# Two network blocks on one core: convolution taps on TensorE column groups, score masks added by VectorE

## The chip, the cores and the metric

The kernel runs on one core of one Trainium2 chip. Its time is device microseconds of one execution; three runs of the kernel before gave 2316.55, 2317.32 and 2319.4 us, and the median, 2317.32 us, is the figure that the change is compared with. Besides the timed runs one execution was profiled, and all durations below come from it.

## The reference, cut to what matters

The program takes 256 tokens of width 1024 through four layers. In the first two, each token mixer is a depthwise convolution of 31 taps over 512 channels beside an attention of 8 heads with a relative bias; a dense feed-forward net and a net of 8 experts follow. The last two layers have a differential attention (a), a sparse attention on the 64 best keys (b), and a compressed, selected and windowed attention (c). What the change touches:

```python
# first block, per layer l
z = a * sigmoid(g)                                     # 256 tokens x 512 channels
z = depthwise_conv(z, conv_w[l], left pad 30) + conv_b[l]   # 31 taps per channel
z = silu(layernorm(z, ln_g, ln_b))
s = einsum(q, k) * 64**-0.5 + rel_bias[clip(key - query)]   # 8 heads, chunks of 64
p = softmax(where(valid, s, -1e30));  o = p @ v

# second block, per layer i
p = softmax(where(mask, q @ k.T, -1e30));  o = p @ v   # mask: causal, or the chosen keys
hid = gelu(einsum("bnlgd,ldf->bngf", blocks, w1))      # compressing net, for keys and for values
kc, vc = hid @ w2
```

## The kernel before, in words

All tensors of one token mixer live on chip; weights stream from HBM once, 1 MB at a time, into four raw tiles, and ScalarE and VectorE split each into two parts (`split`, L176 to L181) so that three products in `mm3` (L183 to L186) give float32 accuracy. SyncE issues all loads in one queue in order; a load waits there until a raw tile is free, and everything behind it waits too. A scheduler fixes the order of the instructions of each engine when the program is built, so an engine stands still when its next instruction is not ready.

`mix1` (from L487) is the token mixer of the first two layers. It projects the gated half (ca, cg), then k, q and v, while in layer 0 the modulation of later parts (`ada` loads, L294, and VectorE's sums, L299) runs between. `gated` writes the convolution's input `zp`, channels on partitions, four tiles of 128 channels. Of the 31 taps of each of the four channel tiles, the table `NPE` gives some to TensorE: 0, 0, 16 and 31 in layer 0, and 0, 0, 0 and 31 in layer 1. A tap on TensorE is a product with a diagonal matrix `dg` that ScalarE makes (L584, L585); a tap on VectorE is one multiply and add over 256 tokens (L569). So 78 taps are products and 170 are VectorE's.

The attention goes through the 8 heads in four pairs. `pair_scores` issues the scores (L611, two heads on the two halves of the rows), adds the bias as a product with a matrix that reverses 128 rows (`flip`, L619), takes the row maximum (L626) and the exponential (L627). The bias tile has one buffer, so the bias of the next pair is loaded (L598) once this pair's has been read; the masked corners are filled by GpSimd (L601, L602). `pair_out` transposes and multiplies with v: the two heads' outputs stand in the two halves of the columns (`po`, L649, L650). `ln` (L689 on) and `wo_unit` finish the mixer.

`block2` (from L1245) is one of the last two layers. `scores` (L1323) makes the scores of two heads and adds the mask as a bf16 product with the identity (L1332 causal, L1334 chosen keys); `softmax_e` (L1313) takes maximum and exponential. The compressing net (L1642) multiplies, for keys and then for values, 16 stationary tiles of 32 columns with `w1`. Pieces of the other matrix products (`fill`) are put between, so TensorE has work while a softmax runs.

The lines of the convolution on TensorE:

```python
A.activation(dg, ident, AF.Copy, scale=cw[:, i, j : j + 1])
T.matmul(st["cps", i][:, :S], dg, zp[:, i, j : j + S], start=(j == 0), stop=(j == npe[i] - 1))
```

Of the kernel before, what the change touches and what calls it, by code (L numbers as in the profile page):

```python
# [24 lines left out]
KT = 8  # L25
# [7 lines left out]
NPE = ((0, 0, 16, 31), (0, 0, 0, 31))  # taps of the convolution on TensorE, by layer and channel tile  # L33
# [3 lines left out]
# columns of the packed per-partition vectors  # L37
# [27 lines left out]
# columns of the second block's w_in  # L65
# [8 lines left out]
def kernel(ctx: ExitStack, tc: tile.TileContext, I: dict, out: bass.AP, dbg=None, upto=99):  # L74
# [3 lines left out]
    # ------------------------------------------------------------- pools  # L78
# [15 lines left out]
    # --------------------------------------------------------- constants  # L94
# [14 lines left out]
    identb = const.tile([P, P], BF16, name="identb")  # L109
    G.tensor_copy(identb, ident)  # L110
    # additive causal mask of a diagonal block: key (free) after query (partition)
# [3 lines left out]
    # the permutation that reverses 128 rows  # L115
    flip = const.tile([P, P], F32, name="flip")
    G.memset(flip, 0.0)
    G.affine_select(flip, flip, pattern=[[1, P]], compare_op=ALU.not_equal, fill=1.0, base=-127, channel_multiplier=1)
    # strictly upper ones: row token before column token
# [22 lines left out]
    ahead = {}  # weights whose loads were started early  # L142
# [47 lines left out]
    def fill(n=1):  # L190
        """Emits the next pieces of matrix products that wait for nothing here."""
# [9 lines left out]
    later = []  # what follows a product, once the next piece's matrix products are out  # L201
# [69 lines left out]
    def transpose4(src, cols):  # L271
        """PSUM [128, 512] with the transposes of src[:, t, cols[i]] at i*256 + t*128."""
# [54 lines left out]
    def mod_parts(l, accp):  # L327
        """Closures of pieces of the six parts of the modulation, by part; each part fills its entry of the dict."""
# [21 lines left out]
    def square(c, ts=(0, 1)):  # L350
        """The sums of squares of one half of x's columns, as soon as that half is done."""
# [8 lines left out]
    def rstd_cols(name, ts=(0, 1)):  # L360
        """1/sqrt(mean(x^2)+eps) of the token tiles ts, each as its own column."""
# [14 lines left out]
    def rsqrt_cols(v, name, ts=(0, 1)):  # L376
        """As rsqrt, of v[:, 0, 0:2], for a short chain: each column by itself with per-partition scalars."""
# [17 lines left out]
    def mod_first(m, accp):  # L395
        """The first norm's shift (on TensorE) and scale (on VectorE) by quarters of the columns, as norm_mod asks for them."""
# [51 lines left out]
    def norm_mod(pool, name, Ac, Bc, before=None):  # L448
        """K-major (x*rstd)*A+B in two parts."""
        rstd, sq = rstd_cols(name)  # L450
        xn = nrm.tile([P, 2, D], F32, tag="xn", name=name + "xn")
# [6 lines left out]
        hT = [pool.tile([P, KT, S], F32R, tag="hT" + "hl"[i], name=name + "hl"[i]) for i in range(2)]  # L458
# [22 lines left out]
    def split_psum(dst, sl, ps):  # L481
        """Both parts of a PSUM result into K-major (or any) tiles dst = [hi, lo]."""
# [3 lines left out]
    def mix1(l, mp, m, fillers, before=None):  # L486
        w_in = I["w_in"][l]  # L487
        npe = NPE[l]
# [10 lines left out]
        # --- gated half for the convolution  # L499
        cv = mp.tile([P, 4, S], F32, tag="cv", name=f"cv{l}")  # L500
        zp = mp.tile([P, 4, S + TAPS - 1], F32, tag="zp", name=f"zp{l}")
        cw = vc(f"cw{l}").rearrange("p (a j) -> p a j", a=4)

        def gated(psg):
# [5 lines left out]
            G.memset(zp[:, :, 0 : TAPS - 1], 0.0)  # L510
            for i in range(0, 4, 2):
                ps = transpose4(z, [i * P, (i + 1) * P])
                A.activation(
                    zp[:, i : i + 2, TAPS - 1 :], ps.rearrange("p (a b) -> p a b", a=2), AF.Identity, scale=0.5
# [3 lines left out]
        grp("cg", 512, gated)  # L518

        # --- queries, keys and values  # L520
# [30 lines left out]
        for i in range(0, 4, 2):  # L551
            ps = transpose4(st["k"], [i * P, (i + 1) * P])
            A.activation(kT[:, i : i + 2, :].rearrange("p a b -> p (a b)"), ps, AF.Identity, scale=vc(f"kg{l}"))
            ps = transpose4(st["q"], [i * P, (i + 1) * P])
            V.tensor_scalar(
                qT[:, i : i + 2, :].rearrange("p a b -> p (a b)"), ps, vc(f"qg{l}"), 0.125, op0=ALU.mult, op1=ALU.mult
            )

        # --- depthwise convolution: some channel tiles on VectorE, the others as diagonal matrices on TensorE
        def conv_v(q):  # L560
            """A third of VectorE's taps, each tap over the channel tiles in turn."""
            todo = [(i, j) for j in range(TAPS) for i in range(4) if j >= npe[i]]
            for i, j in todo[len(todo) * q // 3 : len(todo) * (q + 1) // 3]:
                if j == npe[i]:
                    V.tensor_scalar(
                        cv[:, i, :], zp[:, i, j : j + S], cw[:, i, j : j + 1], vc(f"cb{l}", i, 1), op0=ALU.mult, op1=ALU.add
                    )
                else:
                    V.scalar_tensor_tensor(  # L569
                        cv[:, i, :], zp[:, i, j : j + S], cw[:, i, j : j + 1], cv[:, i, :], op0=ALU.mult, op1=ALU.add  # L570
                    )
            if q == 2:
                for i in range(4):
                    if 0 < npe[i] < TAPS:
                        V.tensor_tensor(cv[:, i, :], cv[:, i, :], st["cps", i][:, :S], op=ALU.add)

        def conv_t(q):
            """A third of TensorE's taps."""
            todo = [(i, j) for i in range(4) for j in range(npe[i])]
            for i, j in todo[len(todo) * q // 3 : len(todo) * (q + 1) // 3]:  # L580
                if j == 0:
                    st["cps", i] = mmps(f"cvp{l}{i}")
                dg = mp.tile([P, P], F32, tag="dg", name=f"dg{l}{i}{j}", bufs=4)
                A.activation(dg, ident, AF.Copy, scale=cw[:, i, j : j + 1])  # L584
# [1370 lines left out]
```

## Time and profile before

| what | value |
|---|---|
| median of three runs | 2317.32 us (2316.55 to 2319.4) |
| span of the profiled execution, first to last instruction | 2314.4 us |
| mean granted TensorE clock | 0.990 |
| TensorE busy, matmul | 2240.5 us, 97% of the span |
| VectorE busy | 1836.1 us, 79% |
| ScalarE busy | 1427.7 us, 62% |
| GpSimd busy | 19.5 us, 1% |
| HBM read | 579.37 MB |

The profiled execution's own time is not listed apart from its span; the span is 2.9 us below the median of the timed runs, which is what lies before the first and after the last instruction together with the difference between executions. Busy time is the time in which an engine worked on something, overlaps counted once. A float32 product shows in the trace as two records on TensorE and two weight loads; a product of one part by one part (`mm3`) and a transpose as one.

### The profile page before, as it was taken

The numbers are of one execution on the slowest core, as the hardware profiler recorded it, in microseconds if no ns is written. First come the engines' busy times: TensorE is split into PE (matmuls) and PEld (weight loads), VectorE is DVE, ScalarE is ACT, GpSimd is POOL, SyncE is SP. The second block draws the span as 40 slices with busy tenths as digits, with TensorE's granted clock in tenths as the row PEclk, the third lists the DMA queues.
The fourth block names the chain that finished last, engine by engine and source line by source line (L and its number), as shares of the span: only waits on it lengthen the run. The fifth ranks groups of instructions, "written<-read, shape, count | busy, mean of one in ns | idle before, by whom it ended". The sixth has DMA issues, their size and how long they took to land. (4 is left out here: it accounts for less than half of the span.)

```text
span 2314.4 us, 28960 instructions
## 1 busy us (share of the span) xinstructions
PE 2240.5 (97%) x10546; PEld 1762.8 (76%) x10546; DVE 1836.1 (79%) x2875; ACT 1427.7 (62%) x2251; POOL 19.5 (1%) x67
## 2 busy tenths in 40 slices
PE   7998998998999999999999999999999999999998
PEld 4776877777877777777778777777777777777776
DVE  7988787887988888888888888986766667766676
ACT  4465344567677767677777767676565546565554
POOL 0000000000000000000000000000000000000000
PEclk9999999999999999999999999999999999999999
DMA  9747886526999999999999999995444346444332
GB/s 337 275 130 280 301 309 225 182 77 218 348 342 337 341 341 360 344 330 343 366 340 348 342 348 357 337 349 199 146 149 147 110 144 186 146 145 140 134 123 91
DMA packets 273452, 582.38 MB, mean 252 GB/s; under 512 B 21644, under 2 KB 41228, under 8 KB 273302
## 3 DMA queue, kind: packets, MB, share of 16 engines
q1 hardware_dynamic: 273302, 580.46, 71.0%
q8 instruction: 85, 1.39, 0.2%
q14 instruction: 65, 0.53, 0.1%
HBM read 579.37 MB, written 1.05 MB: 251 GB/s over the span
## 5 line engine op out<-in xcount | busy, mean ns | idle before, releaser
L299 DVE SCALAR_TENSOR_TENSOR acc<-ada,cact,acc 128x1024 f32<-128x1024 f32 x80 | 102.3, 1280 | 0.9
L483 ACT CAST at<-t 128x512 fp32r<-128x512 f32 x56 | 32.9, 587 | 86.7 <-PE t L1103 86.7
L569 DVE SCALAR_TENSOR_TENSOR cv<-zp,vec,cv 128x256 f32<-128x256 f32 x164 | 70.7, 476 | 0.0
L484 DVE TENSOR_TENSOR at<-t,at 128x512 fp32r<-128x512 f32 x56 | 38.4, 685 | 15.8 <-ACT at L483 15.7
L1320 ACT ACTIVATE ec<-sc,nmc 128x128 f32<-128x128 f32 (+1 forms) x64 | 26.5, 417 | 27.5 <-DVE nmc L1319 25.9
L356 ACT ACTIVATE sqj<-x 128x512 bf16<-128x512 f32 x36 | 22.5, 625 | 29.4 <-DVE x L479 10.6
L585 PE MATMUL cvp<-zp,dg 128*128 128x256 f32 x156 | 39.1, 391 | 0.0
L584 ACT ACTIVATE dg<-ident,vec 128x128 f32<-128x128 f32 x78 | 27.4, 399 | 18.2 <-DVE x L479 14.7
L585 PEld LDWEIGHTS cvp<-zp,dg 128*128 128x128 f32 x156 | 28.9, 193 | 5.4 <-ACT dg L584 0.9
L1063 ACT ACTIVATE gh<-g,mcol,mcol 128x256 f32<-128x256 f32 x32 | 18.2, 570 | 17.9 <-PE g L1053 17.9
L427 PE MATMUL mq<-ada,cact 128*1 128x256 f32 x64 | 17.0, 427 | 9.9 <-DMA ada<-in_w_ada_dram 9.9
L1319 DVE TENSOR_REDUCE nmc<-sc 128x1 f32<-128x128 f32 (+1 forms) x64 | 20.6, 353 | 5.8 <-ACT ec L1320 3.3
L1053 PEld LDWEIGHTS g<-pm,xnt 128*128 128x128 f32 x128 | 20.4, 206 | 4.3 <-issue 2.0
L1053 PE MATMUL g<-pm,xnt 128*128 128x256 f32 x128 | 21.3, 299 | 1.9 <-DVE pm L1045 1.9
L1319 DVE TENSOR_REDUCE nma<-sa 128x1 f32<-128x128 f32 (+1 forms) x32 | 10.4, 351 | 16.0 <-PE sa L1332 13.6
L1127 ACT ACTIVATE yh<-y,ws 128x512 fp32r<-128x512 f32 x14 | 8.9, 685 | 20.9 <-PE y L186 20.9
L427 PEld LDWEIGHTS mq<-ada,cact 128*1 128x1 f32 x64 | 5.6, 91 | 19.9 <-ACT sqj L356 9.3
L619 PE MATMUL s<-bias,flip 128*128 128x128 f32 (+1 forms) x64 | 15.8, 367 | 4.3 <-POOL bias L601 3.7
L627 ACT ACTIVATE sbig<-s,nm 128x128 f32<-128x128 f32 (+1 forms) x32 | 13.2, 415 | 9.6 <-DVE nm L626 9.4
L1147 DVE TENSOR_TENSOR yacc<-yacc,sc 128x512 f32<-128x512 f32 x28 | 19.0, 679 | 0.0
L1320 ACT ACTIVATE eb<-sb,nmb 128x128 f32<-128x128 f32 (+1 forms) x32 | 13.1, 417 | 9.2 <-DVE nmb L1319 8.7
L1347 DVE TENSOR_SCALAR ec<-ec,smc 128x128 f32<-128x128 f32 x64 | 18.1, 313 | 0.8
(4855 smaller groups left out, 8315.6 us busy)
## 6 DMA issues: line engine op xcount, KB each, us to landing
ada<-in_w_ada_dram SPq DMA_DIRECT2D x48, 1024.0 KB, 6.9
bias<-in_rel_bias_dram SPq DMA_DIRECT2D x8, 256.0 KB
x<-in_x_dram SPq DMA_DIRECT2D x1, 1024.0 KB, 4.9
ca0k0r<-in_w_in_dram SPq DMA_DIRECT2D x1, 1024.0 KB
ca0k4r<-in_w_in_dram SPq DMA_DIRECT2D x1, 1024.0 KB
cg0k0r<-in_w_in_dram SPq DMA_DIRECT2D x1, 1024.0 KB
cg0k4r<-in_w_in_dram SPq DMA_DIRECT2D x1, 1024.0 KB, 5.1
k0k0r<-in_w_in_dram SPq DMA_DIRECT2D x1, 1024.0 KB
```

The source lines that it names most:

```text
L299: V.scalar_tensor_tensor(acc, raw[:, k * D : (k + 1) * D], cact[:, k0 + k : k0 + k + 1], acc, op0=ALU.mult, op1=ALU.add)
L356: squares["last"] = A.activation(junk, x[:, t, c * 512 : (c + 1) * 512], AF.Square, accum_out=squares["ss"][:, t, c : c + 1])
L427: T.matmul(ps[0:1, :256], cact[:, k : k + 1], raws[0][:, k, :], start=(k == 0), stop=(k == KT - 1))
L483: A.copy(dst[0][sl], ps)
L484: V.tensor_tensor(dst[1][sl], ps, dst[0][sl].bitcast(F32), op=ALU.subtract)
L569: V.scalar_tensor_tensor(cv[:, i, :], zp[:, i, j : j + S], cw[:, i, j : j + 1], cv[:, i, :], op0=ALU.mult, op1=ALU.add)
L584: A.activation(dg, ident, AF.Copy, scale=cw[:, i, j : j + 1])
L585: T.matmul(st["cps", i][:, :S], dg, zp[:, i, j : j + S], start=(j == 0), stop=(j == npe[i] - 1))
L1053: T.matmul(gp[:, i * S : (i + 1) * S], xn[part][:, t, (k + i) * P : (k + i + 1) * P], pm[:, t].rearrange("p a b -> p (a b)"), start=(n == ...
L1147: last = V.tensor_tensor(a_, a_, ps, op=ALU.add)
L1319: V.tensor_reduce(nm[:, t : t + 1], ps[:, SL[t]], axis=AX.X, op=ALU.max, negate=True)
L1320: A.activation(e[:, SL[t]], ps[:, SL[t]], AF.Exp, bias=nm[:, t : t + 1], accum_out=sm[:, t : t + 1])
```

## The change

The convolution goes to TensorE as a whole, with 4 taps x 32 channels as the 128 rows of one product. `stack` copies `zp` by 16 DMAs into a tile whose four groups of 32 partitions hold the same 32 channels shifted by 0, 8, 16 and 24 tokens; `ident4` and the weights `w4` give stationary tiles of 128 rows x 32 columns (`conv_w`, VectorE). A channel tile is then 8 steps of four products, one for each group of 32 output channels, which stand on the four column groups of the array. In all these are 256 products of 256 columns and 16 VectorE instructions, in place of 78 products, 78 diagonal matrices and 171 VectorE instructions. The two stacks of a layer reuse tiles of the normalization (`xn`, `hTl`); they are issued by SyncE in 2 x 16 DMAs per layer.

Bias and masks are no longer products: one VectorE instruction per head and token tile adds them to the scores, writes the negated sum to SBUF and gives its minimum (`tensor_tensor_reduce`), and the exponential reads SBUF. The queries of `mix1` are stored reversed, so the bias needs no reversal. The compressing net puts keys and values and two halves of the sum on four column groups, and adds the halves on VectorE. The output products of a pair are issued head by head in turn.

```diff
-NPE = ((0, 0, 16, 31), (0, 0, 0, 31))
+TQ = 8
+SW = S + TQ - 1
...
+    ident4 = const.tile([P, TQ, 32], F32, name="ident4")
...
+        def stack(i):
+            if i == 0:
+                z4 = nrm.tile([P, KT * S + 8 * TQ], F32, tag="xn", name=f"zst{l}0")
+            else:
+                z4 = mp.tile([P, KT * S + 8 * TQ], F32R, tag="hTl", name=f"zst{l}1")
...
+            for g in range(4):
+                for t in range(4):
+                    nc.sync.dma_start(
+                        z4[32 * t : 32 * (t + 1), g], zp[32 * g : 32 * (g + 1), i : i + 2, TQ * t : TQ * t + SW]
+                    )
...
         grp("cg", 512, gated)
+        stack(0)
...
+        def conv(i):
+            ws = conv_w(i)
+            ps = mmps(f"cvp{l}{i}")
+            for j in range(TQ):
+                for g in range(4):
+                    T.matmul(
+                        ps[32 * g : 32 * (g + 1), :S],
+                        ws[j // (TQ // 2)][:, g, j % (TQ // 2), :],
+                        zst[i][:, g, j : j + S],
+                        start=(j == 0), stop=(j == TQ - 1),
+                    )
+            A.activation(cv[:, i, :], ps[:, :S], AF.Identity, bias=vc(f"cb{l}", i, 1))
...
-                for i in range(2):
-                    T.matmul(pss[i][:, SL[t]], flip, bias[:, i, SL[t]], start=False, stop=True)
...
-                    V.tensor_reduce(nm[:, t : t + 1], pss[i][:, SL[t]], axis=AX.X, op=ALU.max, negate=True)
+                    V.tensor_tensor_reduce(
+                        out=s[:, SL[t]], in0=pss[i][:, SL[t]], in1=bias[:, i, SL[t]], scale=-1.0, scalar=3e38,
+                        op0=ALU.add, op1=ALU.min, accum_out=nm[:, t : t + 1],
+                    )
...
                 ess[a + 1] = pair_scores(a + 1)
-                conv_t(a)
-                conv_v(a)
+                if a == 0:
+                    stack(2)
+                    conv(0)
+                conv(a + 1)
...
-                        T.matmul(ps[:, t * S : t * S + P], identb, trib, start=False, stop=True)
-                        T.matmul(ps[:, SL[t]], identb, selb[:, SL[t]], start=False, stop=True)
...
-            for jj in range(16):
+        for jj in range(0, 16, 2):
+            for q in range(4):
                 T.matmul(
-                    ph[:32, :P],
+                    ph[32 * q : 32 * (q + 1), :P],
...
-                    stop=(jj == 15),
+                    stop=(jj == 14),
```

On TensorE, in the attention of layer 0 before, from the second pair's scores on (`s` scores and bias, `cvp` the convolution):

```order
L611 MATMUL s_877<-kT_812,qT_813 128x128
L611 MATMUL s_878<-kT_812,qT_813 128x128
L585 MATMUL cvp_905<-zp_354,dg_906 128x256
L585 MATMUL cvp_905<-zp_354,dg_909 128x256
L585 MATMUL cvp_905<-zp_354,dg_912 128x256
L585 MATMUL cvp_905<-zp_354,dg_915 128x256
L611 MATMUL s_1004<-kT_812,qT_813 128x128
L585 MATMUL cvp_905<-zp_354,dg_918 128x256
L585 MATMUL cvp_905<-zp_354,dg_921 128x256
L619 MATMUL s_877<-bias_872,flip 128x128
L619 MATMUL s_878<-bias_872,flip 128x128
L611 MATMUL s_877<-kT_812,qT_813 128x256
```

The same place in the changed kernel (`pt` transposes, `zst` the stacks):

```order
L649 MATMUL s_926<-kT_865,qT_866 128x128
L649 MATMUL s_927<-kT_865,qT_866 128x128
L649 MATMUL s_926<-kT_865,qT_866 128x256
L649 MATMUL s_927<-kT_865,qT_866 128x256
L618 MATMUL cvp_971<-zst_567,cw_967 32x256 x16
L618 MATMUL cvp_971<-zst_567,cw_969 32x256 x16
L618 MATMUL cvp_1009<-zst_567,cw_1005 32x256 x16
L618 MATMUL cvp_1009<-zst_567,cw_1007 32x256 x16
L680 MATMUL pt_1047<-ident,sbig_891 128x128 x3
L680 MATMUL pt_1053<-ident,sbig_891 128x128 x3
L649 MATMUL s_1071<-kT_865,qT_866 128x128
L688 MATMUL po_1059<-pT_1051,v_785 64x256
```

The bias products are gone, and two channel tiles of the convolution, 64 products, stand in one piece behind the second pair's scores.

On SyncE's queue, in the projections of layer 0 before (`ada` modulation weights; k0, q0, v0 the weights of k, q and v):

```order
L153 DMA k0k4r<-in_w_in_dram 128x4x512
L294 DMA ada_614<-in_w_ada_dram 128x2x1024
L153 DMA q0k0r<-in_w_in_dram 128x4x512
L294 DMA ada_652<-in_w_ada_dram 128x2x1024
L153 DMA q0k4r<-in_w_in_dram 128x4x512
```

The same place in the changed kernel:

```order
L160 DMA k0k4r<-in_w_in_dram 128x4x512
L533 DMA zst_567<-zp_384 32x2x263 x16
L301 DMA ada_667<-in_w_ada_dram 128x2x1024
L160 DMA q0k0r<-in_w_in_dram 128x4x512
L301 DMA ada_705<-in_w_ada_dram 128x2x1024
L160 DMA q0k4r<-in_w_in_dram 128x4x512
```

The 16 copies of the first stack, which wait for `zp`, stand ahead of four loads of weights. In layer 1 they come behind the last load of v.

On the same queue, at the end of layer 0's projections before (`wo` the weights of the output projection):

```order
L294 DMA ada_1107<-in_w_ada_dram 128x2x1024
L153 DMA wo040r<-in_w_out_dram 128x4x512
L153 DMA wo041r<-in_w_out_dram 128x4x512
L598 DMA bias_872<-in_rel_bias_dram 128x2x128
L598 DMA bias_872<-in_rel_bias_dram 128x2x256
L153 DMA wo000r<-in_w_out_dram 128x4x512
```

The same place in the changed kernel:

```order
L301 DMA ada_1133<-in_w_ada_dram 128x2x1024
L533 DMA zst_950<-zp_384 32x2x263 x7
L636 DMA bias_921<-in_rel_bias_dram 128x2x128
L636 DMA bias_921<-in_rel_bias_dram 128x2x256
L533 DMA zst_950<-zp_384 32x2x263 x9
L636 DMA bias_1066<-in_rel_bias_dram 128x2x128
L636 DMA bias_1066<-in_rel_bias_dram 128x2x256
L160 DMA wo040r<-in_w_out_dram 128x4x512
```

The second stack waits for the last product of v; the bias of the second and third pair and the loads of `wo` stand behind it.

## Rows read from the trace of the kernel before

**Rows 1.** Busy time by stretch; in brackets the count, then granted clock, DMA share

```profile
69.00:110.00 41.00, 37.20 (x162) 28.89 (x161) 39.14 (x65) 16.53 (x24) 2.31 (x4) 0.96 0.88 303
111.00:158.50 47.50, 44.78 (x243) 33.74 (x242) 41.16 (x97) 37.52 (x110) 2.15 (x7) 1.00 0.41 106
468.10:505.60 37.50, 35.72 (x194) 26.12 (x193) 32.87 (x84) 28.19 (x90) 1.20 (x6) 0.95 0.31 80
1598.00:2314.40 716.40, 701.20 (x3557) 545.29 (x3555) 474.11 (x1125) 393.59 (x830) 0.58 (x5) 1.00 0.42 139
```

**Rows 2.** Groups by line: count, busy us, mean ns of one, idle before them

```profile
L569 DVE SCALAR_TENSOR_TENSOR cv<-zp,vec,cv 128x256 f32<-128x256 f32 x164 | 70.7, 476 | 0.0
...
L1319 DVE TENSOR_REDUCE nmc<-sc 128x1 f32<-128x128 f32 (+1 forms) x64 | 20.6, 353 | 5.8 <-ACT ec L1320 3.3 <-PE sc L1332 2.5
...
L619 PE MATMUL s<-bias,flip 128*128 128x128 f32 (+1 forms) x64 | 15.8, 367 | 4.3 <-POOL bias L601 3.7 <-POOL bias L602 0.6
...
L1642 PEld LDWEIGHTS hidk<-w1k,cb 128*32 128x32 f32 x64 | 6.8, 110 | 0.7 <-issue 0.7
```

**Rows 3.** Timeline of TensorE, first pair's scores and bias in layer 0: start, duration

```profile
111.46 0.71 PE L619 MATMUL s<-bias,flip 128*128 128x128 f32 x4
112.10 0.70 PE L611 MATMUL s<-kT,qT 64*128 64x256 f32 x4
112.73 1.13 PE L619 MATMUL s<-bias,flip 128*128 128x256 f32 x4
113.79 0.49 PE L611 MATMUL s<-kT,qT 64*128 64x128 f32 x4
```

**Rows 4.** Timeline of TensorE, convolution and one pair's outputs in layer 0

```profile
149.81 4.55 PE L585 MATMUL cvp<-zp,dg 128*128 128x256 f32 x20
154.29 0.66 PE L649 MATMUL po<-pT,v 128*64 128x256 f32 x4
154.77 0.40 PE L650 MATMUL po<-pT,v 128*64 128x128 f32 x4
155.10 0.66 PE L689 MATMUL cvT<-ident,cv 128*128 128x128 f32 x4
```

**Rows 5.** Timeline of TensorE, one head's outputs alone in attention c

```profile
1799.61 0.65 PE L1754 MATMUL poc<-pTc,vs 128*64 128x256 f32 x2
...
1800.09 0.38 PE L1755 MATMUL poc<-pTc,vs 128*64 128x128 f32 x2
```

**Rows 6.** Timeline of TensorE, one pair's scores and masks in attention c

```profile
1789.00 0.29 PE L1332 MATMUL sc<-trib,identb 128*128 128x128 bf16 x2
1789.22 0.70 PE L1329 MATMUL sc<-ks,crT 64*128 64x256 f32 x4
1789.85 0.29 PE L1332 MATMUL sc<-trib,identb 128*128 128x128 bf16 x2
1789.95 0.47 PE L185 MATMUL mg000p<-mg000k0l,xT0h 128*128 128x512 f32 x1
```

**Rows 7.** Timeline of TensorE, the compressing net of the third layer

```profile
1764.23 3.68 PE L1642 MATMUL hidk<-w1k,cb 128*32 128x128 f32 x32
1767.75 3.66 PE L1642 MATMUL hidv<-w1v,cb 128*32 128x128 f32 x32
1771.34 0.50 PE L186 MATMUL gc0p<-gc0k0h,xT0l 128*128 128x512 f32 x1
```

**Rows 8.** Timeline of SyncE's queue in the projections of layer 0

```profile
59.40 0.37 SPq L294 DMA_DIRECT2D ada<-in_w_ada_dram  x1
65.72 0.37 SPq L153 DMA_DIRECT2D q0k0r<-in_w_in_dram  x1
```

**Rows 9.** Timeline of ScalarE: the two instructions that write `zp` in layer 0

```profile
67.21 1.08 ACT L513 ACTIVATE zp<-tr 128x512 f32<-128x512 f32 x2 [2.28 <-PE tr L276]
```

**Rows 10.** VectorE's instructions on `cv` alone in a stretch of layer 0

```profile
69.00:110.00 41.00, 0.00 (x0) 0.00 (x0) 9.87 (x22) 0.00 (x0) 0.96 0.88 303
```

**Rows 11.** The loads of the bias, from issue to landing

```profile
DMA to landing us min/median/max: 3.6/3.7/5.3
```

More of the change, by code (lines that the diff above doesn't have):

```diff
@@ L114 @@
     G.affine_select(trib, trib, pattern=[[-1, P]], compare_op=ALU.is_ge, fill=NEG, base=0, channel_multiplier=1)
-    flip = const.tile([P, P], F32, name="flip")
-    G.memset(flip, 0.0)
-    G.affine_select(flip, flip, pattern=[[1, P]], compare_op=ALU.not_equal, fill=1.0, base=-127, channel_multiplier=1)
+    causal = const.tile([P, 384], BF16, name="causal")
+    G.memset(causal[:, P : 2 * P], 0.0)
+    for o in (0, 2 * P):
+        G.tensor_copy(causal[:, o : o + P], trib)
+    ident4 = const.tile([P, TQ, 32], F32, name="ident4")
+    G.memset(ident4, 0.0)
+    for t in range(4):
+        ps_ = slice(32 * t, 32 * (t + 1))
+        for j in range(TQ if t < 3 else TAPS - 3 * TQ):
+            G.tensor_copy(ident4[ps_, j, :], ident[ps_, 32 * t : 32 * (t + 1)])
     upper = const.tile([P, P], F32, name="upper")
@@ L457, in norm_mod @@
         behind.extend([LATE, sq, last])
-        hT = [pool.tile([P, KT, S], F32R, tag="hT" + "hl"[i], name=name + "hl"[i]) for i in range(2)]
+        hT = [pool.tile([P, KT * S + 8 * TQ], F32R, tag="hT" + "hl"[i], name=name + "hl"[i]) for i in range(2)]
+        hT = [h[:, : KT * S].rearrange("p (k s) -> p k s", k=KT) for h in hT]
         for k in range(0, KT, 2):
@@ L577, in conv_t @@
[L577 to L584, printed above, removed]
-                T.matmul(st["cps", i][:, :S], dg, zp[:, i, j : j + S], start=(j == 0), stop=(j == npe[i] - 1))
-                if j == TAPS - 1:
-                    A.activation(cv[:, i, :], st["cps", i][:, :S], AF.Identity, bias=vc(f"cb{l}", i, 1))
+                qT[:, i : i + 2, :].rearrange("p a (t b) -> p (a t) b", t=2)[:, :, ::-1],
@@ new lines, in mix1, with conv_w @@
+                ps.rearrange("p (a b) -> p a b", b=P), vc(f"qg{l}"), 0.125, op0=ALU.mult, op1=ALU.mult,
+            )
+        def conv_w(i):
+            r = []
+            for h in range(2):
+                w = jp.tile([P, 4, TQ // 2, 32], F32, tag="tmp", name=f"cw{l}{i}{h}", bufs=4)
+                j0 = i * TAPS + h * (TQ // 2)
+                V.tensor_tensor(
+                    w,
+                    ident4[:, h * (TQ // 2) : (h + 1) * (TQ // 2), :].unsqueeze(1).to_broadcast([P, 4, TQ // 2, 32]),
+                    w4[:, :, j0 : j0 + TQ // 2].unsqueeze(3).to_broadcast([P, 4, TQ // 2, 32]),
+                    op=ALU.mult,
+                )
+                r.append(w)
+            return r
@@ L1318, in softmax_e, with scores @@
             for t in range(2):
-                V.tensor_reduce(nm[:, t : t + 1], ps[:, SL[t]], axis=AX.X, op=ALU.max, negate=True)
-                A.activation(e[:, SL[t]], ps[:, SL[t]], AF.Exp, bias=nm[:, t : t + 1], accum_out=sm[:, t : t + 1])
+                V.tensor_tensor_reduce(
+                    out=e[:, SL[t]], in0=ps[:, SL[t]], in1=mask[:, SL[t]], scale=-1.0, scalar=3e38,
+                    op0=ALU.add, op1=ALU.min, accum_out=nm[:, t : t + 1],
+                )
+                A.activation(
+                    e[:, SL[t]], e[:, SL[t]], AF.Exp, bias=nm[:, t : t + 1], scale=-1.0, accum_out=sm[:, t : t + 1]
+                )
             V.reciprocal(sm, sm)
             return e, sm
-        def scores(qk, name, selb=None):
+        def scores(qk, name):
             pss = [atps(f"s{name}{n}") for n in range(len(qk))]
@@ L1541, in block2 @@
             halves = [slice(0, 64), slice(64, 128)]
-            pss = scores([(bqT[hs, a, :], bik[hs, 0, :]) for hs in halves], f"b{a}", selb)
-            ers = [softmax_e(ps, f"b{a}{j}") for j, ps in enumerate(pss)]
+            pss = scores([(bqT[hs, a, :], bik[hs, 0, :]) for hs in halves], f"b{a}")
+            ers = [softmax_e(ps, f"b{a}{j}", selb) for j, ps in enumerate(pss)]
             for e, r_ in ers:
@@ L1550, in block2 @@
                 T.matmul(po[hs, 0:S], vv[:, 0, 0:64], pT[:, 0:S], start=True, stop=False)
+            for hs, pT in zip(halves, pTs):
                 T.matmul(po[hs, P:S], vv[:, 1, 0:64], pT[:, S:384], start=False, stop=True)
@@ L1754, in block2 @@
                     T.matmul(po[hs, 0:S], v_[:, 0, :], pT[:, 0:S], start=False, stop=False)
+                for hs, pT in zip(halves, pTs):
                     T.matmul(po[hs, P:S], v_[:, 1, :], pT[:, S:384], start=False, stop=(c == 1))
```

104 lines of the change are left out of this document (50 added, 54 removed).

## The prediction

> **What bounds the kernel now.** I read the busy times by stretch first. In the last two layers TensorE works 701.2 of 716.4 us at full granted clock, VectorE 474 and the DMA engines 42% [rows 1]: there a product that goes is worth its own time, and an instruction moved to VectorE costs nothing as long as its chain stays under the filling products. In the two attentions of the first block TensorE is still the fullest engine, 44.8 of 47.5 and 35.7 of 37.5 us, but VectorE follows with 41.2 and 32.9, and the second runs at a mean clock of 0.95 [rows 1]. The groups by line say which products wait there: those of the bias stood 4.3 us for GpSimd's corner fill behind the bias load [rows 2]. The projections of layer 0 are another case: VectorE 39.1 of 41.0 us, DMA 88%, TensorE 37.2 [rows 1]; loads and splits set the pace. So I price TensorE's part first, from start-to-start times in the timeline, not from durations, since records overlap.
>
> **Part 1, masks of the second block.** One pair's scores have two mask steps, 1789.00 to 1789.22 and 1789.85 to 1789.95, together 0.32 us [rows 6]. There are 4 pairs in a, 4 in b and 8 in c, in two layers 32 pairs: 10.2 us gone. The chosen-key masks of b have twice the columns in one of the steps; I leave them at the same price. In their place VectorE adds the mask within the maximum. The maximum takes 0.353 us [rows 2]; the new instruction also writes its 128 or 256 columns and hands out the minimum, and no row shows it. I bound it by 0.35 and, for two passes over the data, 0.71 us, and take the first, as it reads the same columns. At the upper end the 128 instructions add 46 us to VectorE's 474 of 716, still far from full, so the cover is the filling products; without it each pair would wait some 1.4 us more, 45 us in all. I count 0.
>
> **Part 2, compressing net.** Keys and values take 1764.23 to 1771.34, 7.11 us for 32 products, 0.222 each [rows 7]; two layers make 14.2. Afterwards 16 fours of products stand on four column groups. Does a four cost one product or four? Two column groups are shown: a pair's two heads stand on two halves of the columns, and their four records of 256 columns take 154.29 to 154.77, 0.48 us [rows 4], while one head alone, two records, takes 1799.61 to 1800.09, also 0.48 [rows 5]. Two groups run wholly beside each other. Four do not occur. For a four of 128 columns the bounds are 0.222 (all beside each other) and 0.89 (in turn); the two-group step of the same columns takes 154.77 to 155.10, 0.33 with the change of layout behind it [rows 4], and I take that: 16 x 0.33 = 5.3, a gain of 8.9 (bounds 10.6 and 0).
>
> **Part 3, bias products.** Per pair 111.46 to 112.10 and 112.73 to 113.79, 1.70 us [rows 3]; 8 pairs, 13.6 us. The output products that are now issued in turn gain nothing, since rows 4 show them beside each other already.
>
> **Part 4, convolution.** 20 records of 10 products take 149.81 to 154.29, 0.448 us each [rows 4]; 78 are 34.9 us. Afterwards there are 64 fours of the same columns. Bounds: 0.448 and 1.79. By the two-group rows a four should cost hardly more than one product; I take 0.50 for twice as many weight loads in the same time: 32.0 us, a gain of 2.9 (bounds +6.2 and -79.8). VectorE loses its taps, 70.7 us [rows 2]; 16 instructions for the weights come instead. ScalarE's diagonal matrices go as well.
>
> **Part 5, waits in those attentions.** The 4.3 us at the bias leave TensorE [rows 2]; the clock of 0.95 over 37.5 us is another 1.9 [rows 1]. What is late next is the chain of the single bias buffer: four maxima (1.4 to 2.8 us), two issues of 0.37 each [rows 8], by the issues of other loads, a landing of 3.7 [rows 11], 5.8 to 7.2 us per pair. Three such reloads, 17 to 22 us, and the last pair's softmax fit under the 33 us of products that are left to each layer, though not by much. I take back half, 3.0 us, of 6.2. The attentions then keep 85.0 - 13.6 - 2.9 - 3.0 = 65.5 us.
>
> **Part 6, SyncE's queue.** This is the price. In layer 0 the 16 copies of the first stack stand ahead of a modulation load that was issued at 59.40 and of q0k0r at 65.72 [rows 8]. They wait for `zp`, whose first half ends at about 67.8 [rows 9], and 16 issues of 0.37 are 5.9: q0k0r cannot leave before 74.0, 8.3 us late, with the DMA engines idle in between. Against that VectorE, the fullest engine of 69 to 110, loses 9.87 us of convolution there [rows 10], and four loads are then issued at once. Bounds: +8.3, and -3.8 (all of TensorE's idle time of the stretch, 41.0 - 37.2, won back). I take +4.0. In layer 1 these copies come behind the last load of v and cost nothing. The second stack holds the bias of the second pair for 7 issues, 2.6 us; 64 products of the convolution cover it. The loads of `wo` behind it are needed only after the attention. Four loads of `w4` per layer, 1.5 us of issuing, and GpSimd's small copies at the start lie before anything that waits for them.
>
> **The sum.** -10.2 - 8.9 - 13.6 - 2.9 - 3.0 + 4.0 = -34.6 us, on the span of 2314.4: 2279.8. The span stands 2.9 us under the median of the timed runs, which I keep: 2282.7 us.
>
> **The rivals.**
> - *Column groups overlap two at a time.* The rows show two and no more. A four of the convolution is then 0.90 and one of the net 0.44: 64 x 0.40 + 16 x 0.11 = +27, 2310 us. Against it: nothing in the two-group rows shows a full resource.
> - *Column groups of 32 go in turn* (the slower side). 64 x 1.29 + 16 x 0.56 = +92, 2374 us. The change loses from about 1.0 us per four on. The two-group rows speak against it.
> - *The weight loads are not hidden.* A four has eight loads of 32 columns, each 0.110 us [rows 2], on the same rows of the array. If they came one after another and ahead of the products, a four would be 0.88 + 0.448 = 1.33 and 0.88 + 0.222 = 1.10 us: 64 x 0.83 + 16 x 0.77 = +65, 2348 us, slower. Against it: the compressing net of before has 32 loads of 0.110 in the 3.52 us from 1764.23 to 1767.75 [rows 2, 7], which the products' own time fills as well, so they lie beside them.
>
> The Trainium skill (TensorE: Matmul & The Clock Gate, section Part 3) says that weight loads overlap running matmuls only where their row groups differ, which for column groups they never do; by that rule this rival would hold. The trace does not agree, with 0.110 us from product record to product record in the net. The same section gives 2.38 times for three column groups, by which a four of the convolution would be some 0.55 to 0.6 us, an estimate, and the sum about 5 us higher.
> - *The queue costs more.* All 8.3 us stay, the second stack delays the bias of pairs two and three, and in layer 1 two expert loads, which need a raw tile, stand ahead of it: +4.3, and the 6 us of waits and clock of part 5 stay: 2293 us.
>
> **How the numbers follow.** The forecast 0.70, two at a time 0.10, in turn 0.04, loads not hidden 0.04, queue 0.12. The likeliest case by itself runs from 2267 (four at 0.448 and 0.222, all waits won, -3.8 on the queue) to 2297 (four at 0.65, +8.3). The range that leaves out less than 2 in 10 is 2263 to 2310. A difference of 0.2%, 4.6 us, is what a measurement of this kernel can tell from none; faster means below 2312.7, which the forecast, the queue and nearly all of the first rival reach: 0.89. Slower, 0.08, is the two rivals in the middle. The same, 0.03.
>
> **What would show it.** Right: 16 products of `cvp` in some 2 us and a compressing net of 2 to 3.5 us per layer; scores of a pair of the second block without a gap between their two steps; attentions of 30 to 35 us in layers 0 and 1; q0k0r issued at about 75. Wrong: four-product steps of 0.9 us or more; VectorE's new instruction above 0.7 us with TensorE waiting for ScalarE's exponentials; a gap of over 8 us ahead of the products of q0; the wo loads late.

## The result and the profile after

The changed kernel takes 2288.12 us (median of 4 runs, 2286.79 to 2288.83) against 2316.94 for the kernel before (4 runs): a ratio of 0.9875, interval 0.9861 to 0.9889, or 28.8 us less. The profiled execution's span is 2286.3 us, 28.1 below that of before. The forecast was 2282.7, so the sum is close; its terms are less so, as a table of landmarks shows. Each row compares the moment at which TensorE ended the same product in the two traces.

| TensorE ends | before | after | difference |
|---|---|---|---|
| first projection of layer 0 (ca) | 53.1 | 58.5 | +5.4 |
| last product of v, layer 0 | 107.7 | 123.6 | +15.9 |
| second part of wo, layer 0 | 169.9 | 172.7 | +2.8 |
| last product of v, layer 1 | 465.8 | 468.4 | +2.7 |
| second part of wo, layer 1 | 517.2 | 516.4 | -0.8 |
| one early group of expert products | 594.0 | 591.0 | -3.0 |
| scores of b, third layer | 1692.1 | 1687.5 | -4.6 |
| scores of a, third layer | 1740.0 | 1733.4 | -6.6 |
| gate beside the compressing net | 1782.0 | 1770.7 | -11.3 |
| last filling product of attention c, third layer | 1883.1 | 1867.9 | -15.2 |
| the output projection, fourth layer | 2275.4 | 2247.3 | -28.1 |

So almost nothing had been gained by the time the experts begin: the projections of layer 0 lose 15.9 us, its attention and that of layer 1 give them back. The two last layers give 25 of the 28 us.

The busy times by stretch answer [rows 1]. The stretches are the projections of layer 0 up to the attention, the two attentions from the first scores to the last outputs, and the last two layers; columns as there.

```profile
69.00:126.60 57.60, 44.36 (x187) 33.99 (x185) 40.52 (x53) 19.85 (x29) 2.40 (x4) 0.88 0.67 231
127.20:162.60 35.40, 32.33 (x379) 20.66 (x379) 20.64 (x65) 25.59 (x71) 2.16 (x7) 0.95 0.76 210
472.50:504.90 32.40, 28.93 (x358) 17.36 (x357) 13.56 (x66) 20.17 (x65) 1.20 (x6) 1.00 0.41 95
1595.00:2286.30 691.30, 676.38 (x3430) 523.70 (x3428) 471.55 (x1254) 394.22 (x823) 0.58 (x5) 1.00 0.45 144
```

The attentions went from 47.5 and 37.5 to 35.4 and 32.4 us, and VectorE, with 41.2 and 32.9 us there before, is busy for 20.6 and 13.6. In the last two layers TensorE does 676.4 us of work instead of 701.2, and VectorE has not more than before: 471.6 for 474.1. Its instruction with the mask costs what the maximum cost [rows 2], beside a record of 83 ns that reads the minimum out: the groups by line, count, busy time and mean.

```profile
L1361 DVE CUSTOM_DVE_ANT_0 ec<-sc,causal 128x128 f32<-128x128 f32 x64 | 19.7, 352 | 2.0 <-PE sc L1376 2.0
```

The timeline of TensorE in the attention of layer 0, which answers [rows 3, 4]: the scores of two pairs in one piece, then 64 products of the convolution, 128 records.

```profile
127.21 1.58 PE L649 MATMUL s<-kT,qT 64*128 64x128 f32 x16
128.72 7.12 PE L618 MATMUL cvp<-zst,cw 128*32 128x256 f32 x128
135.78 0.87 PE L680 MATMUL pt<-ident,sbig 128*128 128x128 f32 x6
136.58 0.48 PE L649 MATMUL s<-kT,qT 64*128 64x128 f32 x2
140.14 0.81 PE L688 MATMUL po<-pT,v 128*64 128x256 f32 x3 [3.07 <-ACT pT L682]
```

From 128.72 to 135.78 are 16 fours: 0.441 us each, as little as one product of before (0.448). The last row is the wait that is left: 3.07 us for the first pair's probabilities, which ScalarE copies only after the second pair's exponentials.

The compressing net of the third layer answers [rows 7]: its first product, and, from 1759.12 on, its 31 others up to the next piece of the gate.

```profile
1757.66 0.41 PE L1685 MATMUL hid<-w1k,cb 128*32 128x128 f32 x2
1757.99 0.50 PE L193 MATMUL gc0p<-gc0k0h,xT0l 128*128 128x512 f32 x1
...
1759.12 0.30 PE L1685 MATMUL hid<-w1v,cb 128*32 128x128 f32 x1
...
1761.00 0.51 PE L191 MATMUL gc0p<-gc0k0h,xT0h 128*128 128x512 f32 x1
```

0.33 and 1.88 are 2.21 us, where 7.11 stood; within the run a four starts every 0.22 us, as one product did before. The masked scores of attention c answer [rows 6]; the first row is of before and stands ahead of those, the two others are the same place after.

```profile
1788.58 0.49 PE L1329 MATMUL sc<-ks,crT 64*128 64x128 f32 x4
```

```profile
1777.19 0.93 PE L1376 MATMUL sc<-ks,crT 64*128 64x128 f32 x8
1778.04 0.51 PE L192 MATMUL mg000p<-mg000k0l,xT0h 128*128 128x512 f32 x1
```

Before, a pair took from 1788.58 to 1789.95, 1.37 us, 0.32 of them in mask steps. After, it takes 0.85. That is 0.52 less: the score products themselves became 0.20 shorter, though they are the same eight records.

SyncE's queue answers [rows 8]: start of the issue, its length, and how many.

```profile
63.07 0.37 SPq L160 DMA_DIRECT2D k0k4r<-in_w_in_dram  x1
73.21 10.40 SPq L533 DMA_DIRECT2D zst<-zp  x16
83.71 0.53 SPq L301 DMA_DIRECT2D ada<-in_w_ada_dram  x1
84.33 0.43 SPq L160 DMA_DIRECT2D q0k0r<-in_w_in_dram  x1
```

The queue stands still from 63.4 to 73.2, then issues copies for 10.4 us, 0.65 each; q0k0r leaves at 84.33 and not at 65.72. TensorE stands 9.38 us ahead of q's products for it:

```profile
92.97 1.22 PE L191 MATMUL q0p<-q0k0h,n10h 128*128 128x512 f32 x2 [9.38 <-ACT q0k0h L185]
```

The stop goes with a loss of clock. From 87 to 97 us the granted clock was 0.50, its lower level of 1.2 GHz, where it was 1.00 before, and the first eight of q's products stand 0.4 to 0.7 us apart in place of 0.23.

About half of the 5.4 us lost before that is in VectorE's order at the program's start. First before, then after:

```profile
39.54 0.54 DVE L471 TENSOR_SCALAR n10h<-tr,mcol,mcol 128x256 f32<-128x256 f32 x1 [2.57 <-ACT n10h L467]
40.12 0.69 DVE L472 TENSOR_TENSOR n10l<-n10h,n10h 128x512 fp32r<-128x512 f32 x1
40.73 2.60 DVE L299 SCALAR_TENSOR_TENSOR acc<-ada,cact,acc 128x1024 f32<-128x1024 f32 x2
43.74 0.54 DVE L471 TENSOR_SCALAR n10h<-tr,mcol,mcol 128x256 f32<-128x256 f32 x1 [0.41 <-ACT n10h L467]
```

```profile
42.02 0.69 DVE L481 TENSOR_TENSOR n10l<-n10h,n10h 128x512 fp32r<-128x512 f32 x1
45.65 0.54 DVE L480 TENSOR_SCALAR n10h<-tr,mcol,mcol 128x256 f32<-128x256 f32 x1 [2.94 <-ACT n10h L476]
46.23 0.69 DVE L481 TENSOR_TENSOR n10l<-n10h,n10h 128x512 fp32r<-128x512 f32 x1
46.84 2.60 DVE L306 SCALAR_TENSOR_TENSOR acc<-ada,cact,acc 128x1024 f32<-128x1024 f32 x2
49.36 2.35 DVE L186 TENSOR_TENSOR ca0k4l<-ca0k4r,ca0k4h 128x1024 fp32r<-128x1024 f32 x2
```

Two modulation sums that used to fill VectorE's gap now stand behind it, ahead of the split that TensorE waits for: 3.29 us in place of 0.77 in the middle of ca. The scheduler fixed this order when the program was built; the four loads of `w4` are ahead of the modulation weights in the queue. Another 1.9 us had been lost when ca began (at 37.97 and not 36.06), and this differs between executions: e5 and e8 below begin as the changed kernel does and have 36.35 and 36.47 there, e2, which has no `w4`, has 37.98. The rest goes with the granted clock, 0.61 from 48 to 54 us, where it was 0.85.

### The profile page after: what moved, and what is told of

It is laid out like the page before. It is cut to its first block, busy times and chain, and to the rows that moved or that the text cites. A ratio compares the mean times of both kernels' runs of the same rounds, so it can differ in the third digit from the quotient of the medians.

```text
span 2286.3 us, 29302 instructions
## 1 busy us (share of the span) xinstructions
PE 2199.8 (96%) x10708; PEld 1720.0 (75%) x10708; DVE 1779.2 (78%) x2878; ACT 1408.4 (62%) x2171; POOL 24.9 (1%) x101
## 3 DMA queue, kind: packets, MB, share of 16 engines
HBM read 579.80 MB, written 1.05 MB: 254 GB/s over the span
## 5 line engine op out<-in xcount | busy, mean ns | idle before, releaser
L492 ACT CAST at<-t 128x512 fp32r<-128x512 f32 x56 | 32.9, 587 | 86.4 <-PE t L1145 86.3
L1365 ACT ACTIVATE ec<-ec,nmc 128x128 f32<-128x128 f32 x64 | 28.6, 447 | 16.8 <-DVE nmc L1361 16.8
L618 PE MATMUL cvp<-zst,cw 128*32 128x256 f32 x512 | 29.9, 389 | 0.0
L618 PEld LDWEIGHTS cvp<-zst,cw 128*32 128x32 f32 x512 | 16.1, 112 | 13.3 <-issue 2.8
L662 DVE CUSTOM_DVE_ANT_0 sbig<-s,bias 128x128 f32<-128x128 f32 (+1 forms) x32 | 10.3, 354 | 14.6 <-POOL bias L639 6.7
L666 ACT ACTIVATE sbig<-sbig,nm 128x128 f32<-128x128 f32 (+1 forms) x32 | 14.3, 447 | 11.8 <-DVE nm L662 11.8
L1361 DVE CUSTOM_DVE_ANT_0 ec<-sc,causal 128x128 f32<-128x128 f32 x64 | 19.7, 352 | 2.0 <-PE sc L1376 2.0
L1361 DVE CUSTOM_DVE_ANT_0 ea<-sa,causal 128x128 f32<-128x128 f32 (+1 forms) x32 | 10.3, 354 | 13.9 <-PE sa L1376 13.9
L1189 DVE TENSOR_TENSOR yacc<-yacc,sc 128x512 f32<-128x512 f32 x28 | 19.1, 681 | 0.0
L1365 ACT ACTIVATE eb<-eb,nmb 128x128 f32<-128x128 f32 (+1 forms) x32 | 14.3, 446 | 6.9 <-DVE nmb L1361 6.9
L1106 ACT ACTIVATE xg<-g,mcol,mcol 128x256 fp32r<-128x256 f32 x32 | 18.3, 572 | 0.0
L487 DVE TENSOR_TENSOR rtmp<-fd,mrow 128x512 f32<-128x512 f32 x12 | 8.2, 688 | 12.5 <-PE fd L193 12.5
L1389 DVE TENSOR_SCALAR ec<-ec,smc 128x128 f32<-128x128 f32 x64 | 17.2, 317 | 0.6
```

Of the source, the lines that this page charges most:

```text
L492: A.copy(dst[0][sl], ps)
L618: T.matmul(ps[32 * g : 32 * (g + 1), :S], ws[j // (TQ // 2)][:, g, j % (TQ // 2), :], zst[i][:, g, j : j + S], start=(j == 0), stop=(j == ...
L1106: A.activation(xg[0][:, k + i, :], gp[:, i * S : (i + 1) * S], AF.Identity, scale=a_, bias=b_)
L1189: last = V.tensor_tensor(a_, a_, ps, op=ALU.add)
L1361: V.tensor_tensor_reduce(out=e[:, SL[t]], in0=ps[:, SL[t]], in1=mask[:, SL[t]], scale=-1.0, scalar=3e38, op0=ALU.add, op1=ALU.min, accum_o ...
L1365: A.activation(e[:, SL[t]], e[:, SL[t]], AF.Exp, bias=nm[:, t : t + 1], scale=-1.0, accum_out=sm[:, t : t + 1])
```

## The experiments

Theory: masks, net and bias save what their products took; the convolution needs the queue, which costs more than forecast; the sum comes out because the masks gave more. The rival: the forecast's terms hold and the rest is scattered over the program.

**One part at a time.** Four kernels take the kernel before and one part of the change each.

`e1_masks_only`:

```diff
-                V.tensor_reduce(nm[:, t : t + 1], ps[:, SL[t]], axis=AX.X, op=ALU.max, negate=True)
+                V.tensor_tensor_reduce(out=e[:, SL[t]], in0=ps[:, SL[t]], in1=mask[:, SL[t]], scale=-1.0, ...
-                        T.matmul(ps[:, t * S : t * S + P], identb, trib, start=False, stop=True)
```

> The kernel before with one part of the change: the masks of the second block are added by VectorE within the row maximum, all else as before. Theory A (the sum as predicted: only the mask products' own steps go, 0.32 us for each of 32 pairs): about 2307, a gain of 10 us. Theory B (a mask product between two steps of scores also costs the scores a change of array layout, so that the step of a pair's scores falls from 1.37 us before to 0.85 us as in the changed kernel's trace, 0.52 for each pair): about 2300, a gain of 16 to 17 us, and the start-to-start time of the score products falls from 40.9 to some 35 us although their number stays.

Measured: 2301.86 against 2317.07, ratio 0.9939 (0.9925 to 0.9953), 15.2 us less. Theory B. The pair of scores that took 1.37 us takes 0.86 (TensorE's timeline):

```profile
1784.80 0.93 PE L1338 MATMUL sc<-ks,crT 64*128 64x128 f32 x8
1785.66 0.50 PE L189 MATMUL mg000p<-mg000k0l,xT0h 128*128 128x512 f32 x1
```

Summed from start to next start over both layers, the 128 mask records took 11.2 us, near the forecast's 10.2; the 256 score records fell from 40.9 to 35.2. Taking out products of 128 rows between products of 64 rows also took out the changes from and to them. This goes with the rows and not with the type: the four score records of 256 columns took 0.63 us between bf16 masks [rows 6] and 0.63 between float32 bias products of 128 rows [rows 3], and take 0.52 behind other scores; the four of 128 columns fell from 0.42 to 0.33.

`e2_net_only`:

```diff
-                    ph[:32, :P],
+                    ph[32 * q : 32 * (q + 1), :P],
```

> The kernel before with the compressing net alone on four column groups. Theory A (a four of 128 columns costs 0.275 us as in the changed kernel's trace, and nothing waits for it): 14.2 - 4.4 = 9.8 us gained, about 2307. Theory B (the shorter gap leaves the gelu chain of the net uncovered, since fewer products lie between): 5 us or less gained, about 2312.

Measured: 2308.16, ratio 0.9961 (0.9948 to 0.9975), 8.9 us less. Theory A; its products take 4.4 us from start to start in place of 14.2, in both layers together.

`e3_bias_only`:

```diff
-                    T.matmul(pss[i][:, SL[t]], flip, bias[:, i, SL[t]], start=False, stop=True)
+                        out=s[:, SL[t]], in0=pss[i][:, SL[t]], in1=bias[:, i, SL[t]], scale=-1.0, scalar=3e38,
```

> The kernel before with the relative bias added by VectorE in the two layers of the first block; the convolution as before on VectorE and TensorE. Theory A (the products of the bias bound the attention): 13.6 us of products go, about 2303 to 2306. Theory B (with 70.7 us of convolution still on VectorE these attentions go over to VectorE and to the single bias buffer): 3 to 6 us gained, about 2311 to 2314.

Measured: 2315.69 (11 runs), ratio 0.9993 (0.9984 to 1.0002): no difference that can be told. Theory B, and more so than it said. The busy times of the two attentions:

```profile
112.30:161.50 49.20, 41.42 (x213) 30.18 (x212) 41.61 (x114) 38.17 (x110) 2.15 (x7) 0.90 0.40 107
470.60:506.90 36.30, 30.47 (x162) 21.42 (x161) 31.83 (x99) 28.81 (x90) 1.20 (x6) 0.91 0.29 73
```

TensorE's work fell from 80.5 to 71.9 us, the two stretches stayed at 85.5 after 85.0. TensorE, which had waited 4.5 us there before, now waits 13.5: 11.2 for ScalarE (probabilities 5.7, diagonal matrices 5.5) and the rest for VectorE. The granted clock is 0.90 and 0.91.

`e4_conv_only`:

```diff
-                conv_t(a)
-                conv_v(a)
+                if a == 0:
+                    stack(2)
+                    conv(0)
+                conv(a + 1)
```

> The kernel before with the convolution alone as products on four column groups, with its stacked copies and its weights on the load queue; bias, masks and net as before. Theory A (the queue in layer 0 costs 16 us ahead of the attention and the attentions give only a part back): slower than before by 2 to 8 us, about 2319 to 2325. Theory B (VectorE's 70.7 us of taps were what bounded the two attentions, so the convolution's move pays for the queue): 0 to 6 us faster, 2311 to 2317.

Measured: 2325.66, ratio 1.0044 (1.0031 to 1.0058), 8.6 us slower. Theory A, just above its range. v's products end 14.0 us late, the attentions shrink from 85.0 to 79.6.

`e10_bias_and_conv` takes both, which is the change without masks and net.

> The changed kernel with masks and compressing net as before the change, so that only bias and convolution are new. Theory A (the two need each other: bias alone gave 1.4 us, the convolution alone lost 8.6, and what the whole change gave beyond masks and net, 28.9 - 15.2 - 8.9 = 4.8 us, is theirs together): about 2312. Theory B (the parts add, and the rest of the whole change's gain lies in masks and net with the other parts present): 2324.

Measured: 2314.26 (11 runs) against 2316.46, ratio 0.9990 (0.9981 to 0.9999), 2.2 us less. Nearer to A: alone, the two make -1.4 and +8.6; together they shrink the attentions to 68.1 us, and pay for the queue. The whole is then 15.2 + 8.9 + 2.2 = 26.3 of the 28.8 us, the rest being within the intervals.

**The queue.** `e5_stack_late` moves one line, `e6_w4_other_queue` one name.

```diff
         grp("cg", 512, gated)
-        stack(0)
...
         grp("v", 2048, v_done)
+        stack(0)
```

> The changed kernel with the 16 copies of the first stack placed behind the loads of v in the load queue, instead of ahead of four loads of weights. Theory A (the queue is the price: in the changed kernel's trace the copies held it from 73.2 to 83.6 us and q's products came 15.6 us later than before): q's loads leave by 76 us, v's products end some 10 us earlier, and 6 to 10 us stay to the end, 2278 to 2282. Theory B (what the queue costs is hidden: the attention behind it waits for other things anyway and gives the 10 us back, as it did when the changed kernel came from +15.9 at its start to +2.8 at its end): 2286 to 2289.

Measured: 2282.09, ratio to before 0.9848 (0.9834 to 0.9861), 6.0 us less than the changed kernel. Between the theories, at A's lower end. The queue as expected:

```profile
69.05 0.37 SPq L160 DMA_DIRECT2D q0k0r<-in_w_in_dram  x1
...
91.75 14.57 SPq L533 DMA_DIRECT2D zst<-zp  x16
106.37 1.13 SPq L636 DMA_DIRECT2D bias<-in_rel_bias_dram  x2
```

v's products end at 110.4, 13.2 us earlier, and more than half of that is given back. One place shows in TensorE's timeline: it waits for sums of modulation weights, whose loads now stand behind the second stack in the queue.

```profile
140.01 3.57 PE L318 MATMUL mc<-ones,acc 128*128 128x1 f32 x16 [2.88 <-DVE acc L306]
```

`e6_w4_other_queue`:

```diff
-            nc.sync.dma_start(
+            nc.gpsimd.dma_start(
                 w4[32 * t : 32 * (t + 1)],
```

> The changed kernel with the four small loads of the convolution's weights issued by GpSimd instead of by SyncE; VectorE then sums a modulation part in the gap before the last normalized tiles again, as before the change. Theory A (the 5.4 us lost in the first 55 us come from these four loads, 1 us of issue and a changed order on VectorE, and stay to the end): 2283 to 2285. Theory B (they are swallowed by the wait for the stack's copies behind them, since the load queue is held there anyway): 2287 to 2289.

Measured: 2284.13, ratio 0.9858 (0.9843 to 0.9873), 4.0 us less by the medians, though the intervals overlap. VectorE's order is that of before again, and TensorE's wait in the middle of ca is 0.78 us instead of 3.29. Theory A by the medians, with 2.5 us of the 4.0 shown in the trace: ca ends 1.5 us late instead of 5.4, but 3.9 late in e11 below with the same wait of 0.78.

`e9_late_and_other_queue` has both edits.

> The changed kernel with both edits on the load queue together: the first stack's copies behind the loads of v, and the four small loads of the convolution's weights issued by GpSimd. Theory A (two prices in two places, the start and the loads of q; each edit alone gave 6.0 and 4.0 us): they add, about 2278. Theory B (both only let the same attention begin earlier, which waits for the second stack and the bias anyway): not better than the first edit alone, 2281 to 2283.

Measured: 2277.46, ratio 0.9829 (0.9815 to 0.9842), 10.7 less than the changed kernel. Theory A: 6.0 and 4.0 add. From 87 to 97 us the granted clock is 1.00 again, and the stop ahead of q's products is 0.34 us.

`e11_stack_other_queue` keeps the place of the first stack and gives its copies, too, to GpSimd.

```diff
-                    nc.sync.dma_start(
+                    (nc.gpsimd if i == 0 else nc.sync).dma_start(
                         z4[32 * t : 32 * (t + 1), g], zp[32 * g : 32 * (g + 1), i : i + 2, TQ * t : TQ * t + SW]
```

> The changed kernel with the first stack's 16 copies and the convolution's weight loads issued by GpSimd, at their place in the program; the second stack stays on SyncE. Theory A (what costs is that the loads of q wait in line behind copies that wait for the convolution's input; GpSimd is 1% busy and can wait): 2276 to 2280, as with the copies behind the loads of v. Theory B (GpSimd's issues are slower, or its filling of the bias' corners comes late behind them): 2284 or more.

Measured: 2275.19, ratio 0.9818 (0.9804 to 0.9831), 12.9 less than the changed kernel and the lowest median of all, though its interval overlaps that of e9. Theory A and a little more. GpSimd waits 25.8 us for `zp` with only a fill and the corners of the bias behind it, while SyncE's loads go out:

```profile
72.39 2.11 POOL L533 DMA_DIRECT2D zst<-zp  x4 [25.83 <-ACT zp L549]
```

```profile
69.67 0.37 SPq L160 DMA_DIRECT2D q0k0r<-in_w_in_dram  x1
```

The Trainium skill (DMA: Bandwidth & Descriptors, section "Issuing engines are not separate DMA queues") says that starting DMAs from several engines saves only the time of issuing, which is usually small beside the transfer. Here it is not small: of the 18.6 us by which q0k0r left late in the changed kernel, 10.4 were issues. The others show a second saving: what stands behind a waiting copy no longer waits with it.

`e12_both_stacks_other_queue` gives the second stack to GpSimd as well.

```diff
-                    (nc.gpsimd if i == 0 else nc.sync).dma_start(
+                    nc.gpsimd.dma_start(
```

> The changed kernel with both stacks' copies and the convolution's weight loads issued by GpSimd. Theory A (SyncE's queue is what delays the bias of the third and fourth pair and the loads of the output projection, with 11.2 us of the second stack's issues ahead of them in layer 0): 2 to 4 us less than with the first stack alone there, 2271 to 2273. Theory B (GpSimd also fills the corners of the bias; the second pair's now stand behind 13 and 14 copies, some 7 to 8 us, and the exponentials wait for them): 2276 to 2282.

Measured: 2280.11 (2274.72 to 2282.6), ratio 0.9841 (0.9826 to 0.9856). By the median the time is that of B, though the interval overlaps that of e11. B's cause holds only in part: in layer 0 TensorE waits for the copies themselves. The last three leave from 119.87 to 122.97, behind the corner fills on GpSimd, which wait 2.5 and 1.8 us for the bias, and land 6 us after their issue with loads of `wo` in flight, where copies issued at 113 landed after 2.1. In layer 1 TensorE waits for the probabilities.

```profile
129.24 1.92 PE L618 MATMUL cvp<-zst,cw 128*32 128x256 f32 x12 [4.99 <-DMA zst<-zp]
475.46 1.49 PE L688 MATMUL po<-pT,v 128*64 128x256 f32 x4 [4.96 <-ACT pT L682]
```

**The bias buffer.** `e7_bias_two_buffers` puts the bias of the second and fourth pair into a tile that is free by then.

```diff
+            if a % 2 == 0:
                 bias = mp.tile([P, 2, 384], F32, tag="bias", name=f"bias{l}{a}")
+            else:
+                bias = mp.tile([P, 2, 512], F32, tag="stk", name=f"bias{l}{a}")[:, :, :384]
```

> The changed kernel with a second buffer for the bias, so that the bias of the second and fourth pair needn't wait for the maximum of the pair before. Theory A (TensorE's waits ahead of the outputs, 3.1 us in layer 0 and 1.8, 1.3 and 0.3 us in layer 1, come from the reload of the one buffer): 4 to 6 us less, 2282 to 2284. Theory B (they come from the softmax's own chain over VectorE and ScalarE): 2287 to 2289.

Measured: 2290.54, ratio 0.9882 (0.9867 to 0.9897): no gain, as B has it, but not for B's reason. The waits did shrink, from 3.07 to 2.15 us and in layer 1 to one of 2.27:

```profile
139.30 0.80 PE L691 MATMUL po<-pT,v 128*64 128x256 f32 x3 [2.15 <-ACT pT L685]
486.83 1.49 PE L691 MATMUL po<-pT,v 128*64 128x256 f32 x4 [2.27 <-ACT pT L685]
```

The mean clock of the two attentions with the output projection behind them fell, from 0.96 and 1.00 to 0.93 and 0.92 over 40 to 47 us, and the second stack's copies still hold the bias of the third pair (issued at 137.0 in both). What a bias that is never late would give was not shown.

**The column groups.** `e8_conv_group_major` changes the order of two loops.

```diff
-            for j in range(TQ):
-                for g in range(4):
+            for g in range(4):
+                for j in range(TQ):
```

> The changed kernel with the convolution's 32 products of a channel tile in another order: the eight of one column group one after another, then the next group. The products and their results are the same. Theory A (four products run beside each other only because neighbours stand on different column groups): a product takes 0.448 us again, a channel tile 14.3 instead of 3.6 us, 8 tiles 86 us more, about 2374. Theory B (a product of 32 columns is cheaper by itself, whichever group its neighbours use): 2286 to 2290.

Measured, in one run: 2340.21, 52 us more. The timeline of TensorE, same place as above:

```profile
126.75 22.00 PE L618 MATMUL cvp<-zst,cw 128*32 128x256 f32 x128
```

Two channel tiles take 22.0 us in place of 7.1: theory A, with its price too high. In the changed kernel four records start within some 0.03 us of each other and the next four 0.22 us after them; here each record starts 0.215 us after the last, except near a change of group, where two run together. So neighbours on different column groups run at once, all four, and neighbours on the same one in turn.

## Why the prediction held, point by point

- *Masks, -10.2.* Wrong in size: e1 gives 15.2. The step took the mask records' own start-to-start time and left the scores at theirs, which fell by 5.7 us.
- *Compressing net, -8.9.* Right: 8.9 in e2. A four took 4.4 / 16 = 0.28 us, less than the 0.33 taken.
- *VectorE's price, 0.* Right. 0.35 us was the bound taken, and 0.352 the measured mean; reading the minimum out, 0.083 us, was not counted and was covered.
- *Convolution on TensorE, -2.9.* Right as far as full clock goes: 0.441 us a four against 0.50 taken; 64 fours would be 28.2 us. All the rivals on the column groups fell: two at a time, in turn, and weight loads not hidden. On the last, the Trainium skill's rule (TensorE: Matmul & The Clock Gate, section "Part 3: Packing small matmuls") again disagrees with the trace: eight loads of 0.11 us each lie in a four of 0.441. The estimate of 0.55 to 0.6 us for a four, from the speedup in the same section, was too high here.
- *Bias products and waits, -13.6 and -3.0.* The forecast had 65.5 us left for both attentions; 35.4 and 32.4 are 67.8. But the step that gave each part its own price was wrong: e3 shows that the bias alone gives nothing, because TensorE then waited for ScalarE and VectorE; only with the convolution off both does it count (e10).
- *SyncE's queue, +4.0.* This is the term that failed, with bounds of -3.8 to +8.3. v's products came 15.9 us late. The forecast's own sign of being wrong, a gap of over 8 us ahead of q's products, came in at 9.38. Four things were missed: the loads of `w4`, "before anything that waits for them", changed VectorE's order (2.5 us of waiting, 4.0 by the medians in e6); a copy leaves every 0.65 us and not every 0.37 as a weight load; `zp` itself came later by the first loss; and after the stop the granted clock fell, 0.50 from 87 to 97 us. Taking the price away gives 10.7 (e9) to 12.9 us (e11).
- *The sum.* By the landmarks the projections of layer 0 took 11.9 us more than forecast and the attentions gave 2.3 less (17.2 for 19.5); the stages behind the experts' group in the table gave 6.0 more (25.1 for 19.1, of which e1 puts 5.0 on the masks), and 2.2 came from the clock among the experts (below). That accounts for 6.0 of the 6.5 us between -34.6 and the span's -28.1. That the time came within 6 us of the forecast is partly luck, since errors of both signs met; without the last two it would have been about 2296, still within the range. "The queue costs more", the rival at 2293, was right as to the mechanism and still too cheap.

## What to carry to other kernels

Price a product that goes by the step that it stands in, its neighbours included, not by its own records. Before a copy that waits is put into an in-order queue, ask what stands behind it and how long one issue of that kind takes; an idle engine's queue can be the place for it, as long as nothing that waits stands between the copies there (e12). Two parts that unload different engines of one stage can be worth more together than apart (here -1.4 and +8.6 apart, -2.2 together), so test them together before dropping either.

## What the runs showed of the hardware

- Four products of 32 columns on four column groups run wholly at once: 0.441 us for 256 moving columns in float32, as long as one product of the full width; on one group they follow each other by 0.215 us a record (e8).
- A product of 128 rows between float32 score products of 64 rows costs these some 0.20 us, whether it is bf16 or float32: four score records of 256 columns take 0.63 us between two such products and 0.52 behind other scores, four of 128 columns 0.42 up to one and 0.33 up to other scores.
- A copy from SBUF to SBUF of 32 partitions takes 0.59 us of issuing on SyncE at the median (0.53 on GpSimd), and one leaves every 0.65 us; the 14.57 us of the sixteen in e5 hold stops of up to 3 us between them.
- Among the experts the granted clock was 0.77 for some 5 us in the kernel before, and 1.00 at the same place after; the table above shows 2.2 us there. In the kernel before TensorE had stopped twice just ahead of it, for 0.82 and 1.05 us; in the changed kernel once, for 1.26. First before, then after:

```profile
580.00:585.00 5.00, 5.00 (x19) 4.00 (x18) 5.00 (x5) 1.98 (x2) 0.00 (x0) 0.77 0.79 293
```

```profile
579.00:584.00 5.00, 5.00 (x24) 4.14 (x23) 5.00 (x6) 4.11 (x6) 0.00 (x0) 1.00 0.87 323
```

  The kernels with masks or net alone do not gain there (0.0 and -0.6 us), those with a changed first block do (2.0 to 2.6 us). Why TensorE stops another way there is open: nothing in that stage was changed.
